# Filter spectra of both layers in one early pass, and every SBUF pool on a 128-byte boundary

## The chip, the cores and the metric

The kernel runs on one core of one Trainium2 chip. The metric is the device time of one execution in microseconds (us); a kernel is judged by the median of its runs. Beside the timed runs, one execution was recorded by the hardware profiler, and all rows below come from that one.

## The reference

Two layers of a hybrid block over 1024 latent tokens of width 1024, with 256 context tokens in front, in float32. Each layer is adaLN norm, one input projection, four mixers side by side on 256 columns each, output projection, gated residual, and then a squared-ReLU MLP of width 4096:

```python
for l in range(DEPTH):                                   # DEPTH = 2
    lat_gdn, lat_hy, lat_hg, lat_da = _split(modulate(x, ln1_w[l], sh1, s1) @ w_in[l], GROUP_COLS)
    ...                                                  # the same for the context tokens
    o_a, o_a_c = gdn_mixer(...)                          # gated delta rule, chunks of 64
    o_b, o_b_c = hyena_mixer(...)                        # two long convolutions by FFT
    o_c, o_c_c = hgrn2_mixer(...)                        # gated linear recurrence
    o_d, o_d_c = diff_attn_mixer(...)                    # differential attention
    x = x + g1 * (jnp.concatenate([o_a, o_b, o_c, o_d], axis=-1) @ w_out[l])
    x = x + g2 * sq_relu_mlp(modulate(x, ln2_w[l], sh2, s2), mlp_w1[l], mlp_w2[l])
```

The Hyena mixer needs filters that depend on the parameters alone, not on x: a small sine network over positions gives `h`, times an exponential window, and the spectrum of that enters `long_conv_bidir`. The second layer computes the latent tokens only, so it needs only the spectrum of length 1024; the first needs that of length 256 too.

## The kernel before

All tokens are columns (tiles of 128 channels x 512, 512 and 256 tokens), and most products are made in three matmuls of float32r parts (`mm3`: high x high, high x low, low x high), lines 259 to 261. The order of work in a layer is written out by hand in `run`: generators yield rough costs, and `mix(lead, fill, ratio)` and `weave` advance a filler by so many units for each unit of the leading generator; the build then reorders instructions of an engine a little within a window. Per layer:

1. The norm (L409), with `fill` at ratio 0.2. In layer 0 the filler is `filters(0, "left")` (L1350), in layer 1 there is none.
2. `mix(part(project), fill, RS[2])` (L1775): the projections `z` and `gk`, with the rest of the filters at ratio 1.0, drained at the end.
3. `mix(self.gdn(l), most())` (L1781): the delta rule leads; its filler `most` first projects `gv` and `gq` (values and queries of the delta rule) up to the next `None`, then `i` to `y2`. `gdn` yields `None` once, before it needs `gv` and `gq`; what is left of them is then run at once. What is left of the filler at the end is drained.
4. `mix(self.hgrn(l), fill, ...)` and then `mix(at[0], fill, RD[l])` (L1804): HGRN2 and attention lead, `rest()` (L1783) fills: the projections `dk`, `dq`, `v`, then `hyena` with the modulations `mods`, then in layer 0 the modulations of layer 1, and last `filters(1)` (L1795). `mix` drains what is left after the last attention step.
5. `tail` (L1546): `oh`/`ol` from the mixers' outputs, the product with `w_out`, the norm, and the MLP in 8 blocks, `hidden` (reads `hh`, `hl`) and `mlp_w2` (reads `fh`, `fl`).

One `filters` pass loads the transform basis `bfl` (2 MB) and the positions `nt01`, loads `h2` from DRAM on POOL's queue (L1367, six transfers), and for each of two filter orders: `w3` by SP, sums on DVE, `wh`/`wl`; per 128 positions two matmuls `pw` (L1396, L1397), a window on ACT (L1399) and two products on DVE (L1401); per output tile three rounds of `pm` (L1413), whose matmuls are `pF` (L1316), a copy on ACT (L1419), adds on DVE (L1421, L1423), four adds on POOL (L1433 to L1436), and a store on SP's queue (L1437).

SBUF pools grow from the left, or from the right with `side="right"`. Each tile's bytes are rounded up to 32. The pool `const` is leftmost, and two tiles `eps` stand in it; the pools after it begin at byte 26528, which is 32 past a multiple of 128. The right-hand pools end at byte 229344, 96 past one. So in the tail the tiles `fh`, `fl` (pool `tf`, left) start 32 past a multiple of 128, and `hh`, `hl`, `oh`, `ol` (pool `th`, right) and the weights `whi`, `wlo` (pool `tw`, right) 96 past one; modulo 512 the first are 64 below the weights, and the second are level with them.

Of the kernel before, what the change touches and what calls it, by code (L numbers as in the profile page):

```python
# [9 lines left out]
F32 = mybir.dt.float32  # L10
F32R = mybir.dt.float32r
# [229 lines left out]
class K:  # L241
# [42 lines left out]
    def setup(self, es):  # L284
        nc, tc = self.nc, self.tc
        self.cp = es.enter_context(tc.tile_pool(name="const", bufs=1))
        self.dp = es.enter_context(tc.tile_pool(name="scratch", bufs=1, space=DRAM))
        nc.scalar.preload_act_table_set("natural_log_exp_and_others")
        self.h2 = self.dram("hyh2", [2, DEPTH * 64, T])
        self.KS = {}  # L290
        self.c = {}
        self.eps = {}
        for i, v in enumerate((EPS, 64 * EPS)):
            self.eps[v] = self.cp.tile([128, 1], F32, tag=f"eps{i}", name=f"eps{i}")
            nc.vector.memset(self.eps[v], v)
# [1054 lines left out]
    def filters(self, l, side="right"):  # L1350
# [3 lines left out]
        for nm in "lc"[:1 + (l < DEPTH - 1)]:  # L1354
            a, R = (2, 4) if nm == "l" else (1, 2)
            self.KS[l, nm] = self.dram(f"ks{nm}{l}", [128, 2, a, R, 2, 256])
        with tc.tile_pool(name=f"flt{l}", bufs=1, side=side, reuse_waits="tile") as fp, \
                tc.tile_pool(name=f"fltt{l}", bufs=2, side=side, reuse_waits="tile") as tp:
# [3 lines left out]
            bf = {nm: self.basis(fp, "f", nm) for nm in "lc" if (l, nm) in self.KS}  # L1362
            yield 0
            h2 = fp.tile([128, T], F32R, tag="h2", name="h2l")
            for a, n in CHUNKS:
                for x in range(2):
                    nc.gpsimd.dma_start(h2[64 * x:64 * x + 64, a:a + n].bitcast(F32), self.h2[x, 64 * l:64 * l + 64, a:a + n])  # L1367
            tt = nc.vector.tensor_tensor
            for od in range(2):
                w4 = tp.tile([128, 4, 256], F32, tag="X", name="w4")  # L1370
                w3, wpm = w4[:, 0:2], w4[:, 2:4]
                for x in range(2):
                    nc.sync.dma_start(w3[64 * x:64 * x + 64],
                                      self.i["hyw3"][l].rearrange("k (d c) -> k d c", d=2)[:, :, 256 * od:256 * od + 256])
                nc.vector.tensor_add(wpm[:, 0], w3[:, 0], w3[:, 1])
                nc.vector.tensor_sub(wpm[:, 1], w3[:, 0], w3[:, 1])
                wh = tp.tile([128, 512], F32R, tag="wh", name="wh", bufs=1)
                wl = tp.tile([128, 512], F32R, tag="wl", name="wl", bufs=1)
                wf = wpm.rearrange("k s c -> k (s c)")
                nc.scalar.copy(wh, wf)  # L1380
                nc.vector.tensor_tensor(wl, wf, wh.bitcast(F32), ALU.subtract)
                dec = tp.tile([128, 256], F32, tag="dec", name="dec", bufs=1)
                nc.sync.dma_start(dec, self.i["hyd"][l][:, 256 * od:256 * od + 256])
                nc.scalar.activation(dec, dec, AF.Abs)
                for nm, t0, a, R in (("l", 0, 2, 4), ("c", 8, 1, 2)):
                    if (l, nm) not in self.KS:
                        continue
                    ks = self.KS[l, nm]

                    ph = [fp.tile([128, 2, 4, 256], F32, tag=f"p{s}", name=f"p{s}") for s in range(2)]  # L1390
                    for b in range(R):
                        for ai in range(a):
                            ti = t0 + b * a + ai
                            p = self.m("pw3")
                            hs = h2[:, 128 * ti:128 * ti + 128]
                            nc.tensor.matmul(p, hs, wh, start=True, stop=False)  # L1396
                            nc.tensor.matmul(p, hs, wl, start=False, stop=True)  # L1397
                            w = tp.tile([128, 256], F32, tag="win", name="win")
                            nc.scalar.activation(w, dec, AF.Exp, scale=nt01[:, ti:ti + 1])  # L1399
                            for s in range(2):  # L1400
                                nc.vector.tensor_mul(ph[s][:, ai, b], w, p[:, 256 * s:256 * s + 256])  # L1401
                            yield 0.2
                        if b == 0:

                            r = [ph[s][0:1, 0, 0] for s in range(2)]
                            nc.vector.tensor_add(r[0], r[0], r[1])
                            nc.scalar.mul(r[1], r[0], 0.5)
                            nc.scalar.mul(r[0], r[0], 0.5)
                    for s in range(2):
                        for k in range(a):  # L1410
                            X = tp.tile([128, 4, 256], F32, tag="X", name="X")

                            def pm(o0, o1, b0, b1, ri):  # L1413

                                p = self.m("pF")
                                for x, b in enumerate((b0, b1)):
                                    self.fourier(bf[nm], ph[s], a, ri, k, b, p[:, 256 * x:256 * x + 256])
                                c = tp.tile([128, 256], F32, tag="c", name="c")
                                nc.scalar.copy(c, p[:, 0:256])  # L1419
                                if o0 is not None:  # L1420
                                    tt(o0, c, p[:, 256:], ALU.add)  # L1421
                                if o1 is not None:
                                    tt(o1, c, p[:, 256:], ALU.subtract)  # L1423
                            if R == 2:
                                pm(X[:, 0], X[:, 1], 0, 1, s)
                            else:
                                e = tp.tile([128, 2, 256], F32, tag="e", name="e", bufs=1)
                                g = tp.tile([128, 2, 256], F32, tag="g", name="g", bufs=1)
                                pm(e[:, 0], e[:, 1], 0, 2, s)
                                pm(g[:, 0], None, 1, 3, s)  # L1430
                                pm(None, g[:, 1], 1, 3, 1 - s)
                                sg = (ALU.add, ALU.subtract)
# [289 lines left out]
    def run(self):  # L1722
        nc, tc = self.nc, self.tc
        with ExitStack() as es:
# [4 lines left out]
            for l in range(DEPTH):  # L1729
# [10 lines left out]
                with ExitStack() as ls:  # L1740
                    fill = iter(())
                    if l == 0:
                        net, fill = self.filter_net(), self.filters(0, "left")
                        next(fill)
# [32 lines left out]
                    def most():  # L1777
                        yield from part(project)
                        yield None
                        yield from part(project)  # L1780
# [73 lines left out]
```

## Time and profile before

| | |
|---|---|
| median of 3 runs | 4579.12 us (4574.42 to 4579.52) |
| profiled execution: its time | 4573.73 us |
| its span, first to last instruction | 4572.0 us |
| mean granted TensorE clock | 0.929 of full speed |
| TensorE (PE) busy | 4068.5 us, 89% |
| VectorE (DVE), ScalarE (ACT), GpSimd (POOL) busy | 2353.6, 1619.7, 1090.3 us |

A busy share is an average over stages; PEld is the weight load that overlaps PE's matmuls. The ends of matmuls are modelled, so the spacing of matmuls is read from their starts. A row's "idle" is the time its engine did nothing just before it, with the instruction that ended the wait.

### The profile page before, as it was taken

The numbers are of one execution on the slowest core, as the hardware profiler recorded it, in microseconds if no ns is written. First come the engines' busy times: TensorE is split into PE (matmuls) and PEld (weight loads), VectorE is DVE, ScalarE is ACT, GpSimd is POOL, SyncE is SP. The second block draws the span as 40 slices with busy tenths as digits, with TensorE's granted clock in tenths as the row PEclk, the third lists the DMA queues.
The fourth block names the chain that finished last, engine by engine and source line by source line (L and its number), as shares of the span: only waits on it lengthen the run. The fifth ranks groups of instructions, "written<-read, shape, count | busy, mean of one in ns | idle before, by whom it ended". The sixth has DMA issues, their size and how long they took to land. (4 is left out here: it accounts for less than half of the span.)

```text
span 4572.0 us, 81465 instructions
## 1 busy us (share of the span) xinstructions
PE 4068.5 (89%) x33270; PEld 3281.2 (72%) x33270; DVE 2353.6 (51%) x4599; ACT 1619.7 (35%) x3165; POOL 1090.3 (24%) x1101
## 2 busy tenths in 40 slices
PE   4888899887777899999999998799887789999999
PEld 2766787665555688888888777677665567888887
DVE  7567456657886362222222667455667875222222
ACT  3454413433335342121212555513424464212222
POOL 1131110000211433333333221121001115433333
PEclk7999899887888899999999999899887899999999
DMA  5235733345224421111111425634342243111112
GB/s 200 85 94 155 208 102 115 110 148 180 89 84 151 159 65 49 37 38 41 39 37 38 129 81 153 191 121 131 132 170 103 67 137 118 61 49 48 48 49 88
DMA packets 387721, 468.57 MB, mean 102 GB/s; under 512 B 137843, under 2 KB 246515, under 8 KB 385300
## 3 DMA queue, kind: packets, MB, share of 16 engines
q1 hardware_dynamic: 385524, 458.38, 31.4%
q0 software_dynamic: 1824, 4.98, 0.4%
q8 instruction: 262, 4.29, 0.4%
q14 instruction: 111, 0.91, 0.1%
HBM read 343.81 MB, written 119.44 MB: 101 GB/s over the span
## 5 line engine op out<-in xcount | busy, mean ns | idle before, releaser
L255 POOL TENSOR_TENSOR wlo<-wraw,whi 128x512 fp32r<-128x512 f32 x360 | 479.0, 1336 | 743.6 <-ACT whi L254 740.5
L254 ACT CAST whi<-wraw 128x512 fp32r<-128x512 f32 (+1 forms) x480 | 296.7, 619 | 910.2 <-PE pt L260 759.6
L1596 DVE SCALAR_TENSOR_TENSOR tx<-pt,mod,tx 128x512 f32<-128x512 f32 (+1 forms) x360 | 250.7, 697 | 592.3 <-PE pt L261 592.2
L260 PE MATMUL pt<-fl,whi 128*128 128x512 f32 (+1 forms) x1280 | 475.6, 372 | 0.0
L261 PE MATMUL pt<-fh,wlo 128*128 128x512 f32 (+1 forms) x1280 | 475.5, 372 | 0.0
L259 PE MATMUL pt<-fh,whi 128*128 128x512 f32 (+1 forms) x1280 | 475.2, 371 | 0.0
L261 PE MATMUL pt<-hh,wlo 128*128 128x512 f32 (+1 forms) x1280 | 471.3, 368 | 2.8 <-POOL wlo L255 2.8
L260 PE MATMUL pt<-hl,whi 128*128 128x512 f32 (+1 forms) x1280 | 472.0, 369 | 0.0
L259 PE MATMUL pt<-hh,whi 128*128 128x512 f32 (+1 forms) x1280 | 471.3, 368 | 0.4 <-ACT f L1629 0.4
L1630 DVE TENSOR_TENSOR f<-f 128x512 f32<-128x512 f32 (+1 forms) x160 | 150.3, 941 | 622.1 <-ACT f L1629 618.4
L259 PE MATMUL pproj<-hh,whi 128*128 128x512 f32 (+1 forms) x960 | 373.2, 389 | 7.3 <-ACT u L488 6.7
L260 PE MATMUL pproj<-hl,whi 128*128 128x512 f32 (+1 forms) x960 | 360.9, 376 | 0.0
L261 PE MATMUL pproj<-hh,wlo 128*128 128x512 f32 (+1 forms) x960 | 360.4, 375 | 0.0
L255 POOL TENSOR_TENSOR fl<-f,fh 128x512 fp32r<-128x512 f32 (+1 forms) x160 | 191.5, 1198 | 390.3 <-ACT fh L254 390.3
L260 PEld LDWEIGHTS pt<-fl,whi 128*128 128x128 f32 x1280 | 240.3, 188 | 47.1 <-issue 0.2
L259 PEld LDWEIGHTS pt<-fh,whi 128*128 128x128 f32 x1280 | 240.2, 188 | 47.1 <-ACT whi L254 0.2
L261 PEld LDWEIGHTS pt<-fh,wlo 128*128 128x128 f32 x1280 | 240.1, 188 | 47.0 <-issue 0.5
L261 PEld LDWEIGHTS pt<-hh,wlo 128*128 128x128 f32 x1280 | 241.3, 188 | 44.3 <-POOL wlo L255 4.1
L259 PEld LDWEIGHTS pt<-hh,whi 128*128 128x128 f32 x1280 | 241.3, 189 | 41.0 <-ACT f L1629 0.8
L260 PEld LDWEIGHTS pt<-hl,whi 128*128 128x128 f32 x1280 | 241.4, 189 | 40.4 <-issue 0.2
L259 PEld LDWEIGHTS pproj<-hh,whi 128*128 128x128 f32 x960 | 186.2, 194 | 49.4 <-issue 9.6
L1198 ACT ACTIVATE p<-psc,mx 128x1280 f32<-128x1280 f32 (+1 forms) x144 | 178.0, 1237 | 120.9 <-DVE mx L1197 72.1
(380 smaller groups left out, 8317.0 us busy)
## 6 DMA issues: line engine op xcount, KB each, us to landing
wraw<-mlp_w SPq DMA_DIRECT2D x296, 256.0 KB
modw<-mod_w SPq DMA_DIRECT2D x80, 512.0 KB
wraw<-w_cm SPq DMA_DIRECT2D x88, 256.0 KB
wraw<-w_out SPq DMA_DIRECT2D x64, 256.0 KB
kv<-kvd SPq DMA_DIRECT2D x40, 256.0 KB
k<-dk SPq DMA_DIRECT2D x16, 640.0 KB
bfl<-c_hyfl SPq DMA_DIRECT2D x4, 2048.0 KB
modw<-mod_w SPq DMA_DIRECT2D x4, 2048.0 KB
```

Source lines behind the costliest of these rows:

```text
L254: (hi_eng or nc.scalar.copy)(hi, src)
L255: (lo_eng or nc.gpsimd).tensor_tensor(lo, src, hi.bitcast(F32), ALU.subtract)
L259: nc.tensor.matmul(ps, wh, xh, start=start, stop=False)
L260: nc.tensor.matmul(ps, wh, xl, start=False, stop=False)
L261: nc.tensor.matmul(ps, wl, xh, start=False, stop=stop)
L1198: nc.scalar.activation(p[j], A, AF.Exp, bias=mx[:, j:j + 1], accum_out=sm[:, j:j + 1])
L1596: nc.vector.scalar_tensor_tensor(xm, p, G[:, m, v:v + 1], xm, ALU.mult, ALU.add)
L1630: nc.vector.tensor_mul(f, f, f)
```

## The change

Three edits. First, the `eps` tiles (two times 32 bytes) leave `const` for a pool `edge` of 96 bytes at the right-hand end, and a pad of 32 bytes stays in `const`: left pools now begin at byte 26496 and right pools end at 229248, both multiples of 128. Second, `filters()` runs over both layers in one generator, filler of layer 0's norm and first projections, with one load of the basis; `filters(l + 1)` at the end of `rest()` is gone. The body moves unchanged into `spectra`. Third, in layer 0 `gv` and `gq` are projected in step 2, beside the filters and ahead of `gdn`; layer 1 keeps its order.

```diff
+        edge = es.enter_context(tc.tile_pool(name="edge", bufs=1, side="right"))
...
-        for i, v in enumerate((EPS, 64 * EPS)):
-            self.eps[v] = self.cp.tile([128, 1], F32, tag=f"eps{i}", name=f"eps{i}")
-            nc.vector.memset(self.eps[v], v)
+        eps = edge.tile([128, 24], F32, tag="eps", name="eps")
+        nc.vector.memset(eps, EPS)
+        nc.vector.memset(eps[:, 1:2], 64 * EPS)
+        self.eps[EPS], self.eps[64 * EPS] = eps[:, 0:1], eps[:, 1:2]
+        pad = self.cp.tile([128, 8], F32, tag="pad", name="pad")
+        nc.vector.memset(pad, 0.0)
...
-    def filters(self, l, side="right"):
+    def filters(self):
...
+        with tc.tile_pool(name="flt", bufs=1, reuse_waits="tile") as fp, \
+                tc.tile_pool(name="fltt", bufs=2, reuse_waits="tile") as tp:
             yield 0
             nt01 = fp.tile([128, NT], F32, tag="nt01", name="nt01")
             nc.sync.dma_start(nt01, self.i["c_hyt"])
-            bf = {nm: self.basis(fp, "f", nm) for nm in "lc" if (l, nm) in self.KS}
+            bf = {nm: self.basis(fp, "f", nm) for nm in "lc"}
             yield 0
+            for l in range(DEPTH):
+                yield from self.spectra(l, fp, tp, nt01, bf)
+
+    def spectra(self, l, fp, tp, nt01, bf):
...
-                        net, fill = self.filter_net(), self.filters(0, "left")
+                        net, fill = self.filter_net(), self.filters()
...
-                    project = self.project(l, tp, hh, hl, ["z", "gk", None, "gv", "gq", None, "i", "hf", "hb", "hq", "og", "yv", "y1", "y2",
-                                                           None, "dk", "dq", "v"])
+                    names = ["z", "gk"] + (["gv", "gq", None] if l == 0 else [None, "gv", "gq", None])
+                    names += ["i", "hf", "hb", "hq", "og", "yv", "y1", "y2", None, "dk", "dq", "v"]
+                    project = self.project(l, tp, hh, hl, names)
                     mix(part(project), fill, RS[2])

                     def most():
-                        yield from part(project)
+                        if l > 0:
+                            yield from part(project)
                         yield None
                         yield from part(project)
...
-                        if full:
-                            yield from self.filters(l + 1)
```

## Rows read from the trace of the kernel before

**Rows 1.** The page's part 1: busy us, share of the span, instructions.

```profile
PE 4068.5 (89%) x33270; PEld 3281.2 (72%) x33270; DVE 2353.6 (51%) x4599; ACT 1619.7 (35%) x3165; POOL 1090.3 (24%) x1101
```

**Rows 2.** The timeline of PE from layer 0's last scores to its tail.

```profile
1461.62 0.36 PE L1196 MATMUL psc<-k,q 128*128 128x256 f32 x1
...
1496.57 1.43 PE L1250 MATMUL pss<-sq,c_bones 128*128 128x320 f32 x2 [3.17 <-ACT sq L1248]
...
1524.16 0.79 PE L1396 MATMUL pw<-wh,h2l 128*128 128x512 f32 x1 [9.10 <-ACT wh L1380]
...
1532.73 21.30 PE L1316 MATMUL pF<-p,bfl 128*128 128x256 f32 x96 [0.28 <-DVE p L1401]
1555.12 0.49 PE L259 MATMUL pt<-oh,whi 128*128 128x512 f32 x1 [1.09 <-ACT oh L254]
```

**Rows 3.** The same in layer 1.

```profile
3732.86 0.85 PE L1196 MATMUL psc<-k,q 128*128 128x512 f32 x3
...
3753.98 0.79 PE L259 MATMUL pt<-oh,whi 128*128 128x512 f32 x1 [0.73 <-ACT oh L254]
```

**Rows 4.** Busy us by stretch: filters after attention (layer 0); attention to tail (layer 1).

```profile
core 0: us, PE busy (x) PEld busy (x) DVE busy (x) ACT busy (x) POOL busy (x), PEclk, DMA share, GB/s
1478.00:1555.00 77.00, 61.62 (x231) 46.15 (x231) 26.77 (x67) 20.68 (x51) 22.49 (x32) 0.84 0.40 139
3733.00:3754.00 21.00, 14.74 (x176) 11.19 (x176) 9.15 (x21) 11.52 (x25) 0.47 (x2) 0.96 0.30 99
```

**Rows 5.** Groups by line from 1467 to 1555: layer 1's filter matmuls.

```profile
L1316 PE MATMUL pF<-p,bfl 128*128 128x256 f32 x192 | 45.7, 400 | 0.4 <-DVE p L1401 0.3
...
L1396 PE MATMUL pw<-wh,h2l 128*128 128x512 f32 x16 | 11.0, 685 | 15.9 <-ACT wh L1380 9.1 <-DMA h2l<-hyh 4.9 <-ACT wT L1220 0.9
L1397 PE MATMUL pw<-wl,h2l 128*128 128x512 f32 x16 | 9.6, 601 | 0.0
```

**Rows 6.** Busy us by stretch, layer 0, `z` to the end of the delta rule.

```profile
142.00:266.00 124.00, 123.87 (x685) 108.42 (x685) 68.08 (x142) 63.68 (x135) 11.64 (x17) 0.99 0.28 87
266.00:324.00 58.00, 44.09 (x345) 34.71 (x344) 37.24 (x67) 25.84 (x52) 34.85 (x70) 0.91 0.39 109
324.00:704.00 380.00, 341.62 (x3600) 283.67 (x3598) 216.38 (x538) 135.27 (x274) 64.51 (x69) 0.94 0.50 147
704.00:747.00 43.00, 42.04 (x244) 34.89 (x243) 27.31 (x56) 16.14 (x38) 3.89 (x10) 1.00 0.55 176
```

**Rows 7.** Matmuls of L259 alone, 266 to 324: PE, PEld, PEclk, DMA, GB/s.

```profile
266.00:324.00 58.00, 15.98 (x44) 8.14 (x43) 0.91 0.39 109
```

**Rows 8.** Timeline of PE in the tails: first and last of unbroken runs of matmuls.

```profile
3959.77 0.39 PE L259 MATMUL pt<-hh,whi 128*128 128x512 f32 x1
...
3965.21 0.39 PE L259 MATMUL pt<-hh,whi 128*128 128x512 f32 x1
...
4019.69 0.39 PE L259 MATMUL pt<-fh,whi 128*128 128x512 f32 x1
...
4022.49 0.39 PE L259 MATMUL pt<-fh,whi 128*128 128x512 f32 x1
...
1914.41 0.28 PE L259 MATMUL pt<-hh,whi 128*128 128x256 f32 x1
...
1917.17 0.28 PE L261 MATMUL pt<-hh,wlo 128*128 128x256 f32 x1
...
1902.15 0.28 PE L259 MATMUL pt<-fh,whi 128*128 128x256 f32 x1
...
1903.41 0.28 PE L261 MATMUL pt<-fh,wlo 128*128 128x256 f32 x1
```

**Rows 9.** Groups by line and shape, 1700 to 4572: `mlp_w2` products by L259.

```profile
L259 PE MATMUL pt<-fh,whi 128*128 128x512 f32 x1024 | 404.1, 395 | 0.0
...
L259 PE MATMUL pt<-fh,whi 128*128 128x256 f32 x256 | 71.1, 278 | 0.0
```

**Rows 10.** What SP's queue waited for: 142 to 266, then 1455 to 1560.

```profile
SPq L1437 <- POOL X L1436: 33.2, 4, 10.9
...
SPq L1437 <- POOL X L1436: 58.0, 7, 16.9
```

More of the change, by code (lines that the diff above doesn't have):

```diff
@@ L1348, in filter_net @@
                 yield 0.2
-    def filters(self, l, side="right"):
+    def filters(self):
         nc, tc = self.nc, self.tc
[L1354 to L1358, printed above, removed]
+        for l in range(DEPTH):
+            for nm in "lc"[:1 + (l < DEPTH - 1)]:
+                a, R = (2, 4) if nm == "l" else (1, 2)
+                self.KS[l, nm] = self.dram(f"ks{nm}{l}", [128, 2, a, R, 2, 256])
+        with tc.tile_pool(name="flt", bufs=1, reuse_waits="tile") as fp, \
+                tc.tile_pool(name="fltt", bufs=2, reuse_waits="tile") as tp:
             yield 0
@@ L1361, in filters @@
             nc.sync.dma_start(nt01, self.i["c_hyt"])
-            bf = {nm: self.basis(fp, "f", nm) for nm in "lc" if (l, nm) in self.KS}
+            bf = {nm: self.basis(fp, "f", nm) for nm in "lc"}
             yield 0
[L1364 to L1432, printed above, removed]
-                                nc.gpsimd.tensor_tensor(X[:, 0], e[:, 0], g[:, 0], ALU.add)
-                                nc.gpsimd.tensor_tensor(X[:, 2], e[:, 0], g[:, 0], ALU.subtract)
-                                nc.gpsimd.tensor_tensor(X[:, 1], e[:, 1], g[:, 1], sg[s])
-                                nc.gpsimd.tensor_tensor(X[:, 3], e[:, 1], g[:, 1], sg[1 - s])
-                            nc.sync.dma_start(ks[:, od, k, :, s], X[:, :R])
-                            yield 1
```

73 lines of the change are left out of this document (added).

## The prediction

> **What bounds the kernel now.** I read the page's part 1 first: PE is busy 89% of the span, the next engine 51% [rows 1]. So most of the kernel is a stream of matmuls, and moving work about gains only where PE stands idle or goes slowly. Two places are touched by the change. At the end of layer 0's mixers the timeline of PE shows attention's last scores at 1461.62, its last matmul at 1496.57, and then only filter matmuls of layer 1 until the tail's first product at 1555.12 [rows 2]. In layer 1, which has no filters there, the last scores come at 3732.86 and the first product of the tail at 3753.98 [rows 3]. That is 93.5 us against 21.1 us for the same change-over; what is to be seen is that `filters(1)` does not fill attention, it runs after it, with PE busy 61.6 of 77 us and at a granted clock of 0.84 [rows 4]. At the other place, from 142 to 266, PE is busy 123.9 of 124 us at clock 0.99: projections and the filters of layer 0 together leave no room [rows 6].
>
> **The filters of layer 1 leave the end of layer 0.** Without them I expect layer 0 to change over as layer 1 does: 93.5 - 21.1 = 72 us gained. The code behind the tail's start is the same in both layers (loads of `o`, casts, `w_out`), so what is late next is the `oh`/`ol` casts, as they are now. Bounds: at least 57 us, if attention's own end stays at 1496.57 + 1.4 (1555.1 - 1498.0); at most 78, if the few attention steps that the filters now delay come at once. I take 72.
>
> **They arrive in the early pass.** Their matmuls there are 192 `pF` and 32 `pw` [rows 5]. At full clock 96 `pF` take 21.3 us [rows 2], so 192 take 42.6; the `pw` are 512-column matmuls of the kind that takes 233 ns [rows 8], 32 x 0.233 = 7.5. Together 50 us of PE. The other engines have room: in 142 to 266 DVE is busy 68, ACT 64 and POOL 12 of 124 us [rows 6]. As PE is full there, I add the 50 us whole. One load of the 2 MB basis less is hidden and worth nothing.
>
> **`gv` and `gq` go ahead of the delta rule.** Of their 96 products by L259, 44 now run in 266 to 324 [rows 7]; the build had already pulled the others in front of 266. With their two companions and the norm of `gq` that is some 29 us of PE that moves from the delta rule's stage to the early one. PE work that only moves costs nothing if the idle time stays as it is: in 266 to 747 PE is idle 481 - 428 = 53 us, 14 of it in 266 to 324 [rows 6], where the delta rule's first steps wait on POOL, and projections fill there before (`gq`) and after (`i`). It can turn out better, since the 43 us from 704 to 747 are mostly drained projections [rows 6], and with 10 units less filler next to nothing is left to drain: the early stage then grows by 29 + 50 = 79 and the delta rule's shrinks by 43, a cost of 36 us. It can turn out worse: the most is 88 us, what the pass takes now from 1467 to 1555 with almost no cover. I take 50, the packed price, because the stretch it joins is packed to 99.9%.
>
> **The move of the pools.** In the tails every matmul has its weights loaded under the one before it, and the spacing differs by tile at the same clock. With `hh` 24 steps of 512 columns take 5.44 us, 226.7 ns each; with `fh` 12 steps take 2.80 us, 233.3 ns. With 256 columns it is the other way round: `hh` 23 steps in 2.76 us, 120.0 ns, `fh` 11 steps in 1.26 us, 114.5 ns [rows 8]. `hh` lies level with the weights modulo 512 bytes, `fh` 64 below them. After the change the left pools move down by 32 and the right ones by 96, so `fh` comes level too, and `hh` and the weights stay as they are to each other. If the spacing follows that relation, 3 x 1024 matmuls gain 6.6 ns (20.3 us) and 3 x 256 lose 5.5 ns (4.2 us) [rows 9]: 16 us gained. No row shows a tile on a full 128 bytes; the bounds are nothing, if `fh` is slower for its shorter groups of four, and the removal of all excess (last rival). Against the move speaks a rule of the Trainium skill: by "SBUF — State Buffer", section "Specifications (TRN2)", SBUF has cachelines of 16 bytes, and only crossing lines costs. Every start here is a multiple of 32 already, so by that rule the pools' move is worth nothing and the sum is 16 us higher; the two spacings above show that something beyond a 16-byte line matters, but not that it is the address. I take 16 us, as place is what the code of the two loops does not share apart from the length of a group. The new `eps` memsets are three small instructions at the start, where no one waits for them.
>
> **The sum.** The profiled execution took 4573.7 us (span 4572.0). 4573.7 + 50 - 72 - 16 = 4535.7. The median of the runs lies 5.4 us above the profiled execution, so I predict 4541 us.
>
> **Rivals.**
>
> *Places don't matter.* The move of the filters works as above, and `fh` keeps 233 ns: 4541 + 16 = 4557 us. For it: `fh` is read in groups of 4 accumulating steps and `hh` in groups of 8, so place is not the only difference. Against it: the spacing is uniform within a group, where group length has no hand. The page of the Trainium skill named above would give this time.
>
> *The early pass finds less cover.* The filter's steps go from engine to engine, and PE already waited 9.1 us for `wh` at the turn of an order, and 4.9 us for the reload of `h2` [rows 5]; two such turns and one reload are added, and some 3 filter units run when the projections are out (by the yields, 27.2 units of filters less 4 that the norm takes, against 20 of `z` to `gq`). With 70 us in place of 50 the move is even at 72, and the time is 4561 with the pools' gain, 4577 without; I put it at 4570.
>
> *Slower: the filters' stores hold up the weights on SP's queue.* SP issues in order. Each store of a spectrum (L1437) waits there for POOL's last add, 33.2 us in four waits from 142 to 266 and 58.0 us in seven after attention [rows 10]; the loads of the next projection weights are queued behind it, then ACT's cast of them, then PE. Now PE does not feel it, since weights are loaded one unit ahead. With eight more such stores, and three buffers for raw weights, it may. If PE lost those 58 us on top of the 50, the sum would be 4573.7 + 108 - 72 - 16 + 5.4 = 4599 us. It decides once PE's waits there exceed 72 + 16 - 50 = 38 us. Against it: with four waits of up to 10.9 us PE is still busy 123.9 of 124 us.
>
> *Pools on 128 bytes remove all excess.* `hh` needs 226.7 ns for 512 and 120.0 for 256 columns, so a column costs 106.7/256 = 0.417 ns, one period of 2.4 GHz, and 13.3 ns are overhead [rows 8]. If that overhead went with the offset, 512 columns would take 213.3 ns: 3072 x 20.0 ns for `fh`, 3840 x 13.4 for `hh` and `oh` (3 x 320 products, 2 chunks, 2 layers), 768 x 7.8 and 960 x 13.3 for 256 columns are 132 us in the tails in place of 16: about 4425 us. Against it: an overhead that is equal for 256 and 512 columns looks like a cost per matmul, not like the edge of a line.
>
> **How the numbers follow.** Forecast 0.42 (own range 4525 to 4557), places don't matter 0.20, less cover 0.16, slower by SP's queue 0.14, all excess removed 0.08. The likeliest gives 4541. A measurement of this kernel tells about 0.2%, 9 us, from no change, so faster means under 4570, slower over 4588. Faster: 0.42 + 0.17 of the second case + 0.07 of the third + 0.08 = 0.74. Within: 0.03 + 0.08 + 0.03 of the fourth = 0.14. Slower: 0.12, the rest. The range reaches from 4521, where the change-over gains 78 and the early cost is 36 (4573.7 + 36 - 78 - 16 + 5.4), to 4587, where the third case ends with a cost of 80 and no gain from the pools (4573.7 + 80 - 72 + 5.4); it leaves out the fifth case and most of the fourth.
>
> **What would show it.** In the profile after: filter matmuls (L1316's line) in one block that ends near 340, where the delta rule's first matmul stood at 266 before; PE still full up to there; HGRN2's start near 797 in place of 747; the tail's first product about 21 us after attention's last scores; `fh` at 227 and 120 ns. Wrong would be: gaps of PE behind casts of weights that wait for a load (SP's queue), PE idle above 53 us in the delta rule's stage, attention's end set by the modulations in place of the filters, or spacings in the tails that are neither of the two seen now.

## The result and the profile after

The changed kernel takes 4547.09 us (median of 4 runs, 4541.48 to 4555.33) against 4579.32 for the kernel before (4 runs, 4574.42 to 4583.69). The ratio of the two kernels, from all runs, is 0.9940 with a 95% interval of 0.9926 to 0.9953: faster by 27 us (0.6%), between 22 and 34. The two medians by themselves lie 32 us apart. The profiled execution took 4552.19 us with a span of 4550.4, 5 above the median, where that of before lay 5 below its own. Between the two profiled executions the difference is therefore only 21.5 us.

Part 1 of the page after, as [rows 1]:

```profile
PE 4055.7 (89%) x33270; PEld 3290.5 (72%) x33270; DVE 2345.0 (52%) x4600; ACT 1617.6 (36%) x3165; POOL 1079.7 (24%) x1101
```

The number of matmuls is the same. PE's busy time fell by 12.8 of the 21.5 us; the matmuls that became shorter are those of the `fh` loop (below). The other 8.7 us are less idle time.

The change-over of layer 0, as [rows 2]: the timeline of PE from attention's last scores (L1201) to the first products of the tail. In brackets stands the idle time before a row and who ended it.

```profile
1511.70 0.56 PE L1201 MATMUL psc<-k,q 128*128 128x256 f32 x1
...
1524.51 1.43 PE L1255 MATMUL pss<-sq,c_bones 128*128 128x320 f32 x2 [3.17 <-ACT sq L1253]
1528.18 0.76 PE L259 MATMUL pt<-oh,whi 128*128 128x512 f32 x1 [2.24 <-DVE sq L590]
1532.07 0.80 PE L260 MATMUL pt<-ol,whi 128*128 128x512 f32 x1 [3.13 <-POOL ol L255]
...
1540.23 0.50 PE L260 MATMUL pt<-ol,whi 128*128 128x512 f32 x1 [1.78 <-POOL ol L255]
...
1555.59 0.50 PE L259 MATMUL pt<-oh,whi 128*128 128x512 f32 x1 [3.46 <-ACT oh L254]
...
1568.24 0.80 PE L259 MATMUL pt<-oh,whi 128*128 128x512 f32 x1 [5.68 <-ACT whi L254]
```

From last scores to first product it is now 1528.18 - 1511.70 = 16.5 us, where it was 93.5 [rows 2]. Attention itself ends sooner behind its scores: its last matmul starts 12.8 us after them, where it was 35.0. But behind the first product PE stands still four times, 14 us together, for `ol`, `oh` and `whi`; before, PE's waits in the whole stage from 1555 to 1707 came to 5.8 us.

Busy time by stretch, as [rows 4, 6]: the early stage (142 to 374), the delta rule (374 to 775), what is left of the projections (775 to 805), then the tail's first 32 us.

```profile
core 0: us, PE busy (x) PEld busy (x) DVE busy (x) ACT busy (x) POOL busy (x), PEclk, DMA share, GB/s
142.00:266.00 124.00, 123.95 (x682) 108.57 (x681) 68.69 (x145) 64.03 (x135) 14.56 (x22) 0.98 0.28 90
266.00:340.00 74.00, 73.32 (x374) 62.77 (x373) 50.79 (x105) 38.10 (x82) 18.98 (x24) 1.00 0.28 95
340.00:374.00 34.00, 32.77 (x228) 29.39 (x226) 17.36 (x38) 16.14 (x39) 5.98 (x9) 1.00 0.29 93
374.00:775.00 401.00, 360.61 (x3722) 293.78 (x3723) 222.94 (x553) 128.70 (x263) 92.14 (x139) 0.94 0.52 148
775.00:805.00 30.00, 28.18 (x168) 22.90 (x167) 19.16 (x41) 13.61 (x34) 1.47 (x2) 1.00 0.59 185
...
1528.00:1560.00 32.00, 22.00 (x74) 15.97 (x75) 10.58 (x14) 12.29 (x25) 18.05 (x16) 0.82 0.75 244
```

The early stage is full (230.0 of 232 us) although it is 108 us longer. The delta rule with the drained rest leaves PE idle for 431 - 388.8 = 42 us, 53 before. The tail's first 32 us have PE busy 22 and the DMA engines 75%, at 244 GB/s.

The `fh` loop, as [rows 8] and [rows 9]: first and last of unbroken stretches (51 steps of 512 columns, 11 steps of 256), then two groups from 1700 on.

```profile
4007.91 0.39 PE L259 MATMUL pt<-fh,whi 128*128 128x512 f32 x1
...
4019.47 0.39 PE L259 MATMUL pt<-fh,whi 128*128 128x512 f32 x1
...
1866.46 0.28 PE L259 MATMUL pt<-fh,whi 128*128 128x256 f32 x1
...
1867.77 0.28 PE L261 MATMUL pt<-fh,wlo 128*128 128x256 f32 x1
```

```profile
L259 PE MATMUL pt<-fh,whi 128*128 128x512 f32 x1024 | 399.1, 390 | 0.0
...
L259 PE MATMUL pt<-fh,whi 128*128 128x256 f32 x256 | 72.1, 282 | 0.0
```

11.56 us / 51 = 226.7 ns and 1.31 / 11 = 119 ns, where `fh` had 233.3 and 114.5 [rows 8]. These are, within 1 ns, the two spacings that `hh` had.

What the stages took, in us, from the starts in the two profiles (a = the delta rule's first matmul, b = HGRN2's, c = attention's last scores, d = the tail's first product, e = the first hidden activation; 0 and 1 are the layers):

| kernel | a0 | b0 | c0 | c0 to d0 | d0 to e0 | c0 to a1 | a1 to b1 | b1 to c1 | c1 to the end |
|---|---|---|---|---|---|---|---|---|---|
| before | 266 | 747 | 1461.6 | 93.5 | 151.5 | 1217.9 | 463.4 | 590.5 | 838.5 |
| changed | 374 | 805 | 1511.7 | 16.5 | 164.5 | 1149.3 | 463.8 | 596.6 | 829.0 |

So layer 0 gained 77 at the change-over, lost 50 ahead of it, and lost 13 again between the tail's first product and the first hidden activation. From the last scores to the first hidden activation, layer 0's change-over with the wait behind it gained 245.0 - 181.0 = 64 us. The last column is for the most part the pools' gain in layer 1. In between, layer 1's HGRN2 and attention took 6 us more; the last section comes back to that.

One execution of a kernel doesn't fix these marks to the microsecond. In the profiles of the experiments below, attention's last scores come at 1465.0 and 1465.4 where layer 0's order is that of the kernel before, and between 1500.9 and 1514.0 where both passes of the filters and `gv`, `gq` run early. With the two kernels themselves the means are 1464.0 (three profiles) and 1507.3 (nine): the early pass came to some 43 us at that mark, and the 50 of this pair of profiles is a high draw. From there to the first hidden activation it is steadier: 241.8 to 245.0 us in the same three, and 180.2 to 181.9 in the seven without filters behind attention whose tail loads and casts as before, some 62 less.

### The profile page after: what moved, and what is told of

Read it like the earlier page. It is cut to its first block, busy times and chain, and to the rows that moved or that the text cites. A ratio compares the mean times of both kernels' runs of the same rounds, so it can differ in the third digit from the quotient of the medians.

```text
span 4550.4 us, 81444 instructions
## 1 busy us (share of the span) xinstructions
PE 4055.7 (89%) x33270; PEld 3290.5 (72%) x33270; DVE 2345.0 (52%) x4600; ACT 1617.6 (36%) x3165; POOL 1079.7 (24%) x1101
## 5 line engine op out<-in xcount | busy, mean ns | idle before, releaser
L259 PE MATMUL pt<-hh,whi 128*128 128x512 f32 (+1 forms) x1280 | 471.2, 368 | 0.4 <-ACT f L1640 0.4
L259 PE MATMUL pt<-fh,whi 128*128 128x512 f32 (+1 forms) x1280 | 471.2, 368 | 0.0
L259 PE MATMUL pproj<-hh,whi 128*128 128x512 f32 (+1 forms) x960 | 373.2, 389 | 9.7 <-ACT u L493 9.6
L259 PEld LDWEIGHTS pt<-hh,whi 128*128 128x128 f32 x1280 | 241.3, 189 | 41.1 <-ACT f L1640 0.8
L259 PEld LDWEIGHTS pt<-fh,whi 128*128 128x128 f32 x1280 | 241.3, 189 | 41.0 <-ACT whi L254 0.2
L259 PEld LDWEIGHTS pproj<-hh,whi 128*128 128x128 f32 x960 | 186.3, 194 | 50.1 <-ACT u L493 12.1
```

What stands on the lines that cost most here:

```text
L259: nc.tensor.matmul(ps, wh, xh, start=start, stop=False)
```

## The experiments

All ratios are against the kernel before on the same chip; "at 4579" is the ratio times 4579.3. The changed kernel is 4552 on that scale. The expectations in the quoted blocks name its median, 4547, so what an experiment gained or lost is read on the common scale, as a difference from 4552.

### The pools alone

```diff
+        edge = es.enter_context(tc.tile_pool(name="edge", bufs=1, side="right"))
...
-            self.eps[v] = self.cp.tile([128, 1], F32, tag=f"eps{i}", name=f"eps{i}")
...
+        eps = edge.tile([128, 24], F32, tag="eps", name="eps")
...
+        pad = self.cp.tile([128, 8], F32, tag="pad", name="pad")
```

> The kernel before, with the pools' move alone; the filters and gv, gq stay where they were. Theory (the spacing follows the place of the moving tile against the weights, modulo 512 bytes): fh goes from 233 to 227 ns at 512 columns and from 114.5 to 120 at 256, hh and oh stay, and the time falls by the 16 us of the prediction's term, to about 4563. Rival (groups of 4 steps are slower than groups of 8, wherever they lie): fh keeps 233 ns and the time stays within 3 us of before's 4579.

Measured: 4564.22 us (11 runs), ratio 0.9963 (0.9950 to 0.9976), 4562 at 4579: 17 us. The timeline of the same loop, 51 steps again:

```profile
4007.83 0.39 PE L259 MATMUL pt<-fh,whi 128*128 128x512 f32 x1
...
4019.39 0.39 PE L259 MATMUL pt<-fh,whi 128*128 128x512 f32 x1
```

11.56 / 51 = 226.7 ns. The groups of four steps run as fast as the groups of eight once they lie as `hh` does, so the length of a group has no hand in it. The rival falls. The stages say the same without the spread of whole runs: from the first hidden activation of layer 1 to the end it is 686 to 688 us in all ten profiles in which `fh` lies level with the weights, and 696 to 697 in the four in which it doesn't (the kernel before, that kernel with its loads reordered, and the runs without the pools' move and with `fh` 128 above).

### The filters' move without the pools

```diff
-        edge = es.enter_context(tc.tile_pool(name="edge", bufs=1, side="right"))
...
-        eps = edge.tile([128, 24], F32, tag="eps", name="eps")
...
-        pad = self.cp.tile([128, 8], F32, tag="pad", name="pad")
...
+            self.eps[v] = self.cp.tile([128, 1], F32, tag=f"eps{i}", name=f"eps{i}")
```

> The changed kernel without the pools' move; filters in one pass and gv, gq ahead as in the change. Theory: what the filters' move gives is the rest of the whole, about 32 - 16 = 16 us below before, 4563, with fh back at 233 ns. Rival (the pools are worth nothing and the filters' move brings all): 4547, as with the whole change. Rival (the pass is paid in full in the early stage and only the pools gained): 4579.

Measured: 4566.86 us (12 runs), ratio 0.9968 (0.9955 to 0.9981), 4565 at 4579: 15 us. In its groups the 512-column products of `fh` are back at a mean of 395 ns, 390 in the changed kernel. By the ratios, 17 and 15 make 32, and the whole is 27 (22 to 34); with some 6 us of uncertainty on each part they add up within the intervals.

### `gv` and `gq` back in the delta rule's stage

```diff
-                    names = ["z", "gk"] + (["gv", "gq", None] if l == 0 else [None, "gv", "gq", None])
+                    names = ["z", "gk"] + [None, "gv", "gq", None]
...
                     def most():
-                        if l > 0:
-                            yield from part(project)
+                        yield from part(project)
```

> The changed kernel with gv and gq back as filler of the delta rule in layer 0. Theory (work of PE that only moves costs nothing): the delta rule's first matmul some 30 us earlier than 374, HGRN2's start at 805 plus or minus 5, and the time within 5 us of the changed kernel's 4547. Rival (ahead of the delta rule they make its stage shorter by the 11 us of idle time that fell from 53 to 42): 4558. Rival (they only starve the delta rule of filler): 4537.

Measured: 4555.19 us (6 runs), ratio 0.9946 (0.9929 to 0.9963), 4555 at 4579, 3 us above the changed kernel and inside both intervals. The delta rule's first matmul stands at 337 in place of 374, HGRN2's start at 799 in place of 805, and attention's last scores at 1511.7 in both. Projecting them ahead is worth nothing that can be measured. The times alone (3 us, some 10 either way) don't shut out the rival's 11 us; the stages speak against it, since attention's last scores come at the same time with and without the edit.

### On 128 bytes, but not level with the weights

```diff
-        pad = self.cp.tile([128, 8], F32, tag="pad", name="pad")
+        pad = self.cp.tile([128, 40], F32, tag="pad", name="pad")
```

> The changed kernel with the pad in const 128 bytes longer: every pool still begins on a multiple of 128 bytes, but fh now lies 128 above the weights modulo 512 in place of level with them. Theory (the relation modulo 512 counts): fh at 231 to 235 ns for 512 columns, as the projections show now in that relation, and the time 12 to 20 us above the changed kernel, about 4563. Rival (the multiple of 128 counts): fh stays at 227 and the time at 4547.

Measured: 4567.45 us (11 runs), ratio 0.9966 (0.9953 to 0.9980), 4564 at 4579. The timeline of the loop, 51 steps:

```profile
4007.80 0.39 PE L259 MATMUL pt<-fh,whi 128*128 128x512 f32 x1
...
4019.70 0.40 PE L259 MATMUL pt<-fh,whi 128*128 128x512 f32 x1
```

11.90 / 51 = 233.3 ns: all of the pools' gain is gone although `fh` and the weights each begin on a multiple of 128 bytes. The boundary itself does nothing; what counts is how `fh` lies to the weights, as the theory has it. Level is fast, 64 below and 128 above are slow. A distance of 256 was not tried by itself, so whether the spacing repeats after 512 bytes or already after 256 is open. (The change itself puts the outermost pools on such a boundary, and not every pool: some inside them still begin off it.)

### Layer 1's pass of filters left out

```diff
-            for l in range(DEPTH):
-                yield from self.spectra(l, fp, tp, nt01, bf)
+            yield from self.spectra(0, fp, tp, nt01, bf)
+            self.KS[1, "l"] = self.KS[0, "l"]
```

> The changed kernel without layer 1's pass of filters: layer 1's long convolution reads the spectra of layer 0, so its numbers are not those of the reference. Theory (PE is full in the early stage, so the pass is paid with its 50 us of matmuls): the delta rule's first matmul at about 374 - 50 = 324, and the time at about 4497. Rival (the pass finds less cover than that): 70 us gained, 4477. Rival (part of it is hidden): under 35 us gained, above 4512.

Measured: 4507.94 us (4 runs), ratio 0.9846 (0.9830 to 0.9861), 4509 at 4579: 43 us below the changed kernel. The delta rule starts at 320.90 in place of 373.70:

```profile
320.90 0.31 PE L724 MATMUL pg<-g,c_btri 128*128 128x40 f32 x2
```

The pass costs 53 us where it stands, 43 by the time, and 41 by attention's last scores (1471.0 against 1511.7; 36 against the mean of 1507.3). 70 us for less cover falls. It is paid in full in the early stage, and most of it at the end: up to some 10 us may come back on the way. By the time alone (43, some 10 either way) the other rival's bound of 35 isn't shut out.

### The loads of `x` behind those of `w_out`

```diff
-            x = []
-            for k in range(KT):
-                t = xp.tile([128, T], F32, tag=f"x{k}", name=f"tx{k}")
-                nc.sync.dma_start(t[:, :toks], self.X[k][:, :toks])
-                x.append(t)
+            x = [xp.tile([128, T], F32, tag=f"x{k}", name=f"tx{k}") for k in range(KT)]
...
-                    product(self.weight(self.i["w_out"][l, m]), oh, ol, ...)
+                    wt = self.weight(self.i["w_out"][l, m])
+                    if cs == (0,):
+                        nc.sync.dma_start(x[m][:, :toks], self.X[m][:, :toks])
+                    product(wt, oh, ol, ...)
```

> The changed kernel with the eight loads of x (5 KB for each partition) issued in the tail one by one, each behind the weight loads of its w_out block, in place of all of them ahead of the first. Theory (the tail that now starts on attention's heels waits for loads that queue together: o, all of x, then w_out): layer 0 from the tail's first product to the first hidden product goes from 165 us back to about 152, and the time falls by 8 to 13, to about 4537. Rival (the waits there are casts on POOL and ACT): 165 stays and the time stays within 4 us of 4547.

Measured: 4535.54 us (6 runs), ratio 0.9904 (0.9888 to 0.9920), 4535 at 4579: 16 us below the changed kernel. The first product to the first hidden activation takes 153.4 us in layer 0 (164.5) and 117.1 in layer 1 (121.6). SP's queue shows why. Its timeline in the kernel before, then in the changed one, then in this run (time, length, line, what is loaded, how many):

```profile
1509.89 0.38 SPq L1578 DMA_DIRECT2D tx<-xT  x1
...
1519.61 3.98 SPq L1578 DMA_DIRECT2D tx<-xT  x6
```

```profile
1529.17 0.33 SPq L1589 DMA_DIRECT2D tx<-xT  x1
1532.04 2.02 SPq L1584 DMA_DIRECT2D o<-o  x4
...
1555.17 3.40 SPq L1584 DMA_DIRECT2D o<-o  x4
1558.62 1.38 SPq L1589 DMA_DIRECT2D tx<-xT  x3
1560.04 38.01 SPq L270 DMA_DIRECT2D wraw<-w_out  x16
```

```profile
1552.64 0.42 SPq L270 DMA_DIRECT2D wraw<-w_out  x1
1553.12 0.42 SPq L1616 DMA_DIRECT2D tx<-xT  x1
1553.72 2.13 SPq L1584 DMA_DIRECT2D o<-o  x4
1555.90 0.42 SPq L270 DMA_DIRECT2D wraw<-w_out  x1
```

`tx` is `x`, `wraw` are the weights. In the kernel before the eight loads of `x` went out from 1510 to 1524, under the filters, 31 us ahead of the first product. With the filters gone they go out from 1529 to 1560, in between the loads of `o` that the first products need, and the next load of `w_out` is behind them all, at 1560.04. The trace gives 640 KB for each; eight are 5.2 MB, 21 us at the 244 GB/s of that stretch. In this run the build still moved three loads of `x` up, but the next load of `w_out` goes out at 1552.64, and what was the longest wait of the line-up shrinks from 5.68 to 0.81 us:

```profile
1535.36 0.80 PE L260 MATMUL pt<-ol,whi 128*128 128x512 f32 x1 [3.13 <-POOL ol L255]
...
1556.43 0.50 PE L259 MATMUL pt<-oh,whi 128*128 128x512 f32 x1 [0.81 <-ACT whi L254]
```

The Trainium skill, page "DMA: Bandwidth & Descriptors", section "Two DMAs through the same engine are not ordered", says that descriptors within one queue of one engine start in order. The trace shows the order of issue on SP's queue, the load of `w_out` (1560.04) behind the last of `x` (1558.62); when single descriptors started, it doesn't show.

### The subtractions for `ol` on DVE

```diff
-                        self.split(oh[c][k], ol[c][k], raw, lo_eng=nc.vector if k % 2 else nc.gpsimd)
+                        self.split(oh[c][k], ol[c][k], raw, lo_eng=nc.vector)
```

> The changed kernel with all subtractions for ol on DVE, where POOL did every second one. Theory of the loads: at most 3 us gained, 4545. Rival (POOL's subtractions are what the first products wait for): the 5.8 us of PE waits on POOL's ol at the tail's start and some of those that follow go, in both layers, and the time falls by 8 to 12.

Measured: 4542.73 us (6 runs), ratio 0.9923 (0.9904 to 0.9942), 4544 at 4579: 8 us below the changed kernel, the low end of what the rival expected, with intervals that overlap. PE's waits around the change-over (1500 to 1700: line, releaser, us in total, times, longest):

```profile
PE pt L259 <- ACT whi L254: 6.3, 1, 6.3
...
PE pt L259 <- ACT oh L254: 2.9, 1, 2.9
```

5.8 us of waits on POOL's `ol` are gone (1.3 on DVE's stand in their place), and the one on `whi`, which hangs on the load, is no shorter than in the changed kernel (6.3 against 5.7). From first product to first hidden activation it is 160.2 us in layer 0 and 119.8 in layer 1: 4.3 and 1.8 gained, where the order of the loads gave 11.1 and 4.5. POOL is a second and smaller wait at the same place; the theory that gave it at most 3 us was too low.

### The projections' weights level too

```diff
-                    self.nw, self.ww, self.lo_eng = 5, 544, nc.vector
+                    self.nw, self.ww, self.lo_eng = 4, 640, nc.vector
```

> The changed kernel with the projections' weight tiles at 640 words in place of 544, and 4 in place of 5 buffers of the cast weights, for room. At 2176 bytes a tile the weights lie at 0, 128, 256 and 384 against the tokens modulo 512; at 2560 all are level. Theory (spacing by the relation modulo 512, whatever the loop): the projections' 512-column matmuls go from 231 to 235 ns to 227, some 1700 of them by 5.5 ns, 9 us if PE bounds those stages throughout, to about 4539. Rival (the fast spacing belongs to the tails' loops): spacing and time as in the changed kernel, or a few us slower for the missing buffer.

Measured: 4550.78 us (6 runs), ratio 0.9939 (0.9921 to 0.9958), 4551 at 4579, the same as the changed kernel. Unbroken stretches of 23 steps in the early stage, first of the changed kernel, then of this run:

```profile
312.20 0.39 PE L259 MATMUL pproj<-hh,whi 128*128 128x512 f32 x1
...
317.54 0.40 PE L261 MATMUL pproj<-hh,wlo 128*128 128x512 f32 x1
```

```profile
311.67 0.39 PE L259 MATMUL pproj<-hh,whi 128*128 128x512 f32 x1
...
316.91 0.39 PE L261 MATMUL pproj<-hh,wlo 128*128 128x512 f32 x1
```

5.34 / 23 = 232.2 ns and 5.24 / 23 = 227.8 ns. The spacing followed the place in this loop too, and the median did not. Here the tokens `hh` stay at their address and only the weights move, so it is the relation of the two that counts and not the tokens' own address. Layer 0's stages ended where they did (HGRN2 at 805, as in the changed kernel); in layer 1 the delta rule's stage took 458.6 us in place of 463.8, and HGRN2 with attention 602 in place of 597 in this execution. The first difference is real, since in the twelve profiles whose projections' weights lie as in the kernel before the delta rule's stage of layer 1 takes 462.9 to 469.3 us; the second is not, as the last section shows. The missing buffer is a second difference of this run; how much of the gain it took is open.

### 256 columns put 64 bytes below the weights

```diff
+                    if n == 256:
+                        hp.tile([128, 112], F32, tag="padA", ...)      # 448 bytes
                     for y in "hl": got[y, i] = [hp.tile([128, n], F32R, ...) for k in range(KT)]
+                    if n == 256:
+                        hp.tile([128, 16], F32, tag="padB", ...)       # 64 bytes, and the same for fh, fl
```

> The changed kernel with the 256-column tiles of the tail (oh, ol, hh, hl, fh, fl of the context tokens) put 64 bytes below the weights modulo 512, and the 512-column ones left level with them. Theory (256 columns are fastest at 64 below, 512 when level): the 256-column matmuls of layer 0's tail go from 120 to 114.5 ns, 1728 by 5.5 is 9.5 us, to about 4537. Rival (256 columns were fast for something else in the kernel before): 120 ns and 4547.

Measured: 4549.78 us (6 runs), ratio 0.9936 (0.9920 to 0.9953), 4550 at 4579: 2 us, not to be told from none. A stretch of 23 steps, `hh` with 256 columns:

```profile
1905.98 0.28 PE L259 MATMUL pt<-hh,whi 128*128 128x256 f32 x1
...
1908.69 0.28 PE L261 MATMUL pt<-hh,wlo 128*128 128x256 f32 x1
```

2.71 / 23 = 117.8 ns, neither 120.0 nor 114.5. The stage from attention to layer 1's delta rule took 1142.5 us, 6.8 less than in the changed kernel. That gain is real, though the median doesn't show it: from the first hidden activation of layer 0 to layer 1's delta rule it is 962.0 us here, and 967.5 to 969.8 in the eight other profiles with `fh` level that leave the 256-column tiles where they were.

But the place doesn't settle the spacing of 256 columns. `fh` keeps one address through all eight blocks of the MLP. In the last block its 256 columns are multiplied in one long stretch, without 512 columns between them, and there the spacing is another than in the seven blocks ahead. First 71 steps of this run, then of the kernel before:

```profile
2533.20 0.28 PE L259 MATMUL pt<-fh,whi 128*128 128x256 f32 x1
...
2541.26 0.28 PE L261 MATMUL pt<-fh,wlo 128*128 128x256 f32 x1
```

```profile
2562.54 0.28 PE L259 MATMUL pt<-fh,whi 128*128 128x256 f32 x1
...
2570.90 0.28 PE L261 MATMUL pt<-fh,wlo 128*128 128x256 f32 x1
```

8.06 / 71 = 113.5 ns here, where the blocks ahead show 117.7, and 8.36 / 71 = 117.7 in the kernel before, where they show 113.8. So at one address both spacings occur, and the prediction's 114.5 for `fh` held for seven blocks of eight. What decides between them is open.

### The order of the loads in the kernel before

```diff
-                nc.sync.dma_start(t[:, :toks], self.X[k][:, :toks])
...
+                        nc.sync.dma_start(x[m][:, :toks], self.X[m][:, :toks])
```

This is the edit of the run with `x` behind the weights, made to the kernel before.

> The kernel before with the loads of x one by one behind the weight loads of w_out, the edit that gave the changed kernel 16 us. Theory (in the kernel before, the filters after attention covered these loads, so the change brought the wait in layer 0): layer 0 has at most 3 us to gain, from 152 us between the first product and the first hidden activation; layer 1, where no filters ran, gains its 4.5 us; together 4 to 8 us. Rival (the loads of x cost the same with the filters in front): 16 us, as in the changed kernel.

Measured: 4571.19 us (11 runs), ratio 0.9984 (0.9974 to 0.9994): 7 us, as the theory has it. Layer 0 takes 151.2 us from first product to first hidden activation, 151.5 without the edit; layer 1 takes 115.6 in place of 122.0. In layer 1, where nothing covered the loads, the wait is old. In layer 0 the run tests less than the theory asks of it, because the edit does not take hold there: the build moves the loads of `x` up into the filters again, to where they were without the edit.

```profile
1511.16 0.38 SPq L1605 DMA_DIRECT2D tx<-xT  x1
...
1520.81 4.16 SPq L1605 DMA_DIRECT2D tx<-xT  x6
```

That the filters covered these loads rests on the timelines above (1510 to 1524, 31 us ahead of the first product) and on layer 0's 151.5 us, which the changed kernel with reordered loads reaches again but for 2 us.

### Both waits, and all four edits

The first run has the two edits that shorten the tail's start, the second these and the two of place:

```diff
+                        self.split(oh[c][k], ol[c][k], raw, lo_eng=nc.vector)
...
+                        nc.sync.dma_start(x[m][:, :toks], self.X[m][:, :toks])
```

> The changed kernel with the loads of x behind the weight loads, and all subtractions for ol on DVE. Theory (two different waits at the same place): the gains add up but for some 3 us that the second could only take because the first left PE waiting: 16 + 8 - 3 = 21 us below the changed kernel, about 4530. Rival (both shorten one wait): no more than the better of the two, 4537.

Measured: 4529.95 us (5 runs), ratio 0.9894 (0.9880 to 0.9907), 21 us below the changed kernel. From first product to first hidden activation: 151.4 us in layer 0, 112.6 in layer 1. The two waits add up.

```diff
+                        hp.tile([128, 112], F32, tag="padA", name=f"{name}padA")
...
+                    self.nw, self.ww, self.lo_eng = 4, 640, nc.vector
```

> The kernel of the run with x and ol, with the projections' weight tiles at 640 words and four buffers, and the 256-column tiles of the tail 64 bytes below the weights. Theory (the spacings of the projections do not bound their stages; those of 256 columns give 1728 by 2.3 ns, 4 us): 3 to 6 us below that run. Rival (the faster projections now show, since the tail has fewer waits): 10 us below it.

Measured: 4513.30 us (4 runs), ratio 0.9852 (0.9838 to 0.9865), 16.7 us below the run ahead of it on the same chip, and the fastest kernel here, 1.5% below the kernel before. That is more than the theory gave. Two stages carry it: attention to layer 1's delta rule 1128.1 us in place of 1136.3, layer 1's delta rule 458.2 in place of 466.9. Both gains stood in the single runs too (6.8 and 5.2 us), so the rival's reason, that fewer waits uncover the projections, is not shown. Its figure, 10 us, was still nearer than the theory's. The theory took the projections for not bounding their stages, and in layer 1's delta rule they do.

## Why the prediction was right, point by point

The forecast was 4541 us, the median is 4547, and the likeliest case is the one that came. Its steps:

- **The filters leave the end of layer 0: -72.** Up to the tail's first product it was -77 (93.5 to 16.5), near the upper bound of 78: attention's last matmul comes 12.8 us after its last scores in place of 35.0, which is what that bound allowed for. But 13 us of it came back behind the first product, so the change-over as a whole gave 64 (62 over all profiles).
- **"What is late next is the `oh`/`ol` casts, as they are now."** This term was mis-sized: the prediction put its change at nothing, and it was 13 us (151.5 to 164.5 in layer 0). The casts are late for longer, because the loads of `o`, `x` and `w_out` now queue together. The order of the loads returns 11 of the 13, the engine of the subtractions 4, both together 13. Layer 1's change-over [rows 3], which served as the measure, had this wait already, but its rows end at the first product, and the prediction did not look behind it.
- **They arrive in the early pass: +50.** The agreement of the pair of profiles (50.1 us at attention's last scores) is in part luck: over all profiles it is some 43, and the pass taken out alone gives 53 where it stands and 43 by the time, some 10 either way. The reason given, a stage that PE fills, holds: 230.0 of 232 us.
- **`gv` and `gq` ahead: nothing.** Measured 3 us, less than can be told. The early stage grew by 108 us, not 79, because the build pulled most of the projection of `i` forward as well; the delta rule's part shrank in return (HGRN2's start +58, forecast +50), so the sum held. The last filter matmul stands at 369, and not near 340, for the same reason.
- **The pools: -16.** Measured -17 alone. `fh` went from 233.3 to 226.7 ns and from 114.5 to 119, against 120 forecast. The reason stands after the experiments: place, not length of group; level with the weights, not on 128. For 256 columns the reason is not complete, as the run with their offset shows.
- **The sum.** Over all profiles it is 43 - 62 - 16 = -35 us, where the forecast had 50 - 72 - 16 = -38; measured are 32 by the medians and 22 to 34 by the interval. The early pass cost some 7 us less than forecast and the change-over gave some 10 less. That these two misses nearly cancel is luck.

The rivals: that places don't matter fell with the pools alone; the Trainium skill, page "SBUF — State Buffer", section "Specifications (TRN2)", has lines of 16 bytes in SBUF and a penalty for each cross to a new one. By that alone these places would be alike, and here 226.7 and 233.3 ns stand side by side at starts that are all multiples of 128, so the measurement decides against it as a full account. That SP's stores hold up the weights did not come. The queue does wait for them, 78.0 us in 12 waits from 142 to 380, but PE has no wait of more than 0.8 us there that goes by queue or cast of weights in the list of its waits:

```profile
SPq L1448 <- POOL X L1447: 78.0, 12, 20.5
```

```profile
PE pk L765 <- DMA kT<-g: 0.8, 1, 0.8
PE pw L1407 <- ACT wh L1391: 0.6, 1, 0.6
```

So the weights were there in time in spite of the queue. That the buffers ahead of the casts are the reason is likely but not shown. That 128 bytes remove all excess fell: in the tails no stretch of 512 columns came under 226.7 ns, where the rival had 213.3. That an early pass finds less cover fell with the run without it (43, not 70).

## What to carry to other kernels

Work that drains between two stages also covers the loads of the stage behind it. Whoever takes it away gains the time between the stages, and has to look at the queue behind it: what the next stage loads, in which order, and whether what is needed first is issued first. Here reordering eight loads gave 16 us, as much as the pools' move, and more than half of what the whole change gave.

A difference of some nanoseconds in the spacing of matmuls is worth a look at addresses: set the moving tile of 512 columns level with the weights modulo 512 bytes, rather than on a boundary, and count it only in stages that PE bounds.

A gain of 5 us, 0.1%, doesn't show in a median of six runs. It shows in the length of the one stage that the edit touches, when that is laid beside the same stage in all other profiles.

## What the hardware showed beside this

- The spacing of the 512-column matmuls with a weight load each depends on the moving tile's place against the weights: 226.7 to 228 ns in unbroken stretches when level modulo 512 bytes, in three loops (`hh`, `fh` and the projections), 231 to 233 when not (`fh` 64 below and 128 above, the projections at mixed multiples of 128). At 256 columns the values are 119 to 120 level, and at 64 below both 113.5 to 114.5 and 117.8, in one kernel and at one address. Why is not shown by any run here.
- Runs of one kernel spread by 6 to 26 us, and the mean granted clock goes with it. Of 27 executions of the kernel before on one chip the fastest took 4570.23 us at a granted clock of 0.931, and the slowest 4596.65 at 0.925, with 3.2 us for each 0.001 on a line through all 27. The profiled execution of the changed kernel had 0.927, and its two faster runs 0.930 and 0.929 (4541.99 and 4541.48 us).
- The 6 us that layer 1's HGRN2 and attention took longer in the changed kernel can't be put down to an edit. In the fourteen profiles, with the same work in that stretch, it takes 590 to 602 us, and the profile of the kernel before is the shortest of them. The kernel before with its loads reordered, an edit to the tails alone, takes 601. The granted clock of the stretch (a mean over the two levels, 1.2 and 2.4 GHz) is 0.83 to 0.86 and explains little of it: the two lines of the kernel before and of that run have 0.85 both. Below, in this order, the kernel before, the changed kernel and that run.

```profile
3143.00:3733.00 590.00, 477.92 (x6555) 365.00 (x6554) 443.80 (x905) 262.85 (x525) 67.29 (x91) 0.85 0.36 122
```

```profile
3125.00:3721.00 596.00, 482.94 (x6554) 368.08 (x6553) 443.31 (x905) 263.03 (x525) 67.19 (x91) 0.84 0.35 121
```

```profile
3147.00:3748.00 601.00, 486.35 (x6553) 370.65 (x6553) 443.57 (x906) 263.40 (x526) 65.91 (x91) 0.85 0.36 120
```

What sets one execution apart from the next, in its clock or in that stretch, is not shown by these runs.
